# Gate rows spread over the partitions by products with an identity column, in place of 24 one-row transfers

## The chip, the core and the metric

The kernel runs on one core of one Trainium2 chip. The metric is the device time of one execution in microseconds (us). TensorE (PE) multiplies matrices, VectorE (DVE), ScalarE (ACT) and GpSimd (POOL) work element by element, and SyncE (SP) issues all the transfers of this kernel. Each engine takes its own instructions in order and waits for the others by semaphores. PEld is the part of TensorE that loads the stationary operand. TensorE's clock has two levels, 2.4 and 1.2 GHz; the profile gives the granted one as 1.00 and 0.50.

## The reference, cut to what matters

Two blocks of two layers work on 256 latent tokens (x) and 256 context tokens (ctx), each of 1024 features, in float32. The change is in the first block. There the results of a mixer and of a SwiGLU feed-forward (FFN) are normed, multiplied by a gate and added to the stream:

```
m_lat = silu(c) @ ada_w[l] + ada_b[l]          # the same from c_ctx for the context
sh1, sc1, g1, sh2, sc2, g2 = split(m_lat, 6)
x = x + g1 * rmsnorm(y_lat, norm_g[l, 1])      # y_lat: the mixer's result
f = swiglu(rmsnorm(x, norm_g[l, 2]) * (1 + sc2) + sh2, ffn_w_in[l], ffn_w_out[l])
x = x + g2 * rmsnorm(f, norm_g[l, 3])
```

Layer 0 mixes by pooling and a gated recurrence (HGRN) and treats both streams; layer 1 mixes by grouped attention (GQA) and treats the latent stream alone. That makes six gates: g1 and g2 of both streams in layer 0, and g1 and g2 in layer 1. A gate is one row of 1024 values for all tokens of its stream.

## The kernel before

**Weights.** Each large product is three products of split operands (`mm3`, L174 to L177): both operands are cut into a high and a low part. A piece of a weight arrives in a buffer `raw` (transfer at L163), ACT writes its high part `hi` (L151), and DVE, now and then POOL, its low part `lo` (L152). In the first block's layer 0 there are four `raw` buffers and two pairs of `hi` and `lo`; a pair can be rewritten only when TensorE has used it for every token tile.

**Conditions.** The six vectors of a layer lie in a tile `adarows` of 128 partitions by 6 by 256 values (`ada_rows`, L567). Vector v is cut into four pieces of 256 values, and piece j of stream s is on the single partition 32 j + s. Of layer 0, the first norm's scale and shift are made at the start, and the gate g1 and the second norm's two during the mixer; g2 of layer 0 and all of layer 1 are summed on DVE (`ada_apart`, L540: two passes over each piece `adaw` of the weight, L554 and L556, for two streams) while the FFN of layer 0 runs, and one product (L562) adds such a sum over the partitions.

**Gates.** `ada_gate` (L632) makes one gate for use by a token tile, whose tokens are on the partitions. The row must therefore stand on all 128 partitions. It loads the post-norm's gain, a row of DRAM on every partition, into a tile `big`, and copies the four pieces by transfers that read one partition's 256 values 128 times, once for each partition. DVE then multiplies gain and gate:

```
for j in range(4):
    p = 32 * j + s
    self.dma(gate[:, j * 256:(j + 1) * 256], self.adas[l][p:p + 1, 3 * n + 2].unsqueeze(1).to_broadcast([1, P, 256]))
self.V.scalar_tensor_tensor(gate, gain, 32.0, gate, op0=ALU.mult, op1=ALU.mult)
```

The transfers are L638 and the multiplication is L639. The six calls come in pairs at three places: L1652 before the product with `ab_w_out` that ends the HGRN mixer (call it the first place), L1689 in the FFN of layer 0 (second place), and L1713 before the product with `att_w_out` that ends the GQA mixer (third place). The gate is used by `post` (L680): L685 squares a half of a tile's y on ACT, and L686 multiplies y by the gate on DVE. `post_end` (L689) and `prenorm` (L672) follow: the sum of squares becomes a factor (L658, and a power on POOL, L270), L693 adds to the stream, L649, L651 and L652 norm the new stream, L239 transposes it on TensorE, and the scaled transposes are split for the next layer's products.

**Order.** The program's order gives each instruction a priority, and a scheduler sets each engine's order from priorities and estimated times; what it sets is fixed. PSUM tiles are given out by tag in the program's order: the tag `tr` has two banks, `C` one, `A` three and `B` two. All transfers stand in SP's one queue.

Of the kernel before, what the change touches and what calls it, by code (L numbers as in the profile page):

```python
# [17 lines left out]
P = 128  # L18
D = 1024
# [6 lines left out]
# ---------------------------------------------------------------- constants of the shapes alone  # L26
def _constants():
    """One [128, n] float32 array of masks and tables, and where each part lies in it."""
# [3 lines left out]
    # blocks of 1, 2, 4, .. in pairs: the two halves of each pair against each other  # L32
# [49 lines left out]
class Kern:  # L82
    def __init__(self, tc, d, es, stop=None):
        self.tc, self.nc, self.d, self.es, self.stop = tc, tc.nc, d, es, stop
        self.V, self.S, self.G, self.T = tc.nc.vector, tc.nc.scalar, tc.nc.gpsimd, tc.nc.tensor
        self.dma = tc.nc.sync.dma_start
        self.cp = self.pool("cp", 1)
        self.xt = self.pool("xt", 1)
        self.rp = self.pool("rp", 1)
        self.mm = self.pool("mm", 1, space=PSUM)  # L90
        self.n = 0
        self.post_ss, self.post_y = {}, {}
        # two places for a transposed activation [128, 8, 256], as hi and lo
        self.xh, self.xl = (self.t(self.xt, [P, 2, 8, 256], n, F32R) for n in ("xh", "xl"))
        self.place = 1
# [17 lines left out]
    def ps(self, shape=(P, 512), tag="A"):  # L113
        """A bank of PSUM. A tag's tiles are given out in the order of the program."""
        return self.t(self.mm, list(shape), tag, bufs=self.BANKS[tag])
# [7 lines left out]
    def buffers(self, es, raw, split):  # L123
        """Buffers for pieces of weights, for the products that follow."""
# [7 lines left out]
    def low(self):  # L132
        """Instructions that only fill the gaps of others."""
# [6 lines left out]
    def later(self, n):  # L140
        """Instructions that may come after n of those that follow."""
# [4 lines left out]
    # ------------------------------------------------------------ splitting and products  # L146
    spread = False

    def split(self, hi, lo, src, pool=False):
        """hi + lo == src exactly, each with 12 significant bits."""  # L150
# [3 lines left out]
    def piece(self, shape, srcs, perm=None):  # L154
        """A piece of a weight, split: srcs(raw) -> [(part of raw, dram)], of half the piece's second dimension at a time."""
# [24 lines left out]
    def among(self, steps):  # L180
        """A step after each of the products that follow: those of few columns cost the array
        little more than their weights, which are loaded during the others."""
# [6 lines left out]
    def wcols(self, w, c0, n):  # L189
        """[1024, n] columns of a weight as pieces of four chunks of K."""  # L190
# [3 lines left out]
    def tok_major(self, xT, tiles, pcs, n, done, tag=None):  # L194
        """done(tile, psum [tokens, n]) of x @ w for pieces of w, each used for all tiles in turn
        (two at a time if a tag is given)."""
# [12 lines left out]
    def by_tile(self, xT, tiles, jobs, tag=None):  # L209
        """For jobs (pieces of w, columns, done) as in tok_major: all of a tile's products, then the next one's."""  # L210
# [10 lines left out]
    def feat_major(self, xT, w, c0, blocks, done, tag="B"):  # L221
        """done(i, psum [128 features, 256 tokens]) of (x @ w)^T for blocks of 128 columns from c0,
        the banks of tag in turn."""
# [12 lines left out]
    def transposes(self, ps, src, blocks):  # L236
        """ps[:, i] = (block i of src)^T"""
# [3 lines left out]
    def to_xT(self, x, hi, lo, tl, n=8):  # L241
        """Token-major x [128, n*128] into columns tl*128.. of hi, lo [128, n, 256]."""
# [16 lines left out]
    def tiles_of(xT):  # L259
        """Access by (token tile, chunk) to [(hi, lo)] by stream."""  # L260
# [6 lines left out]
    # ------------------------------------------------------------ small things  # L267
# [19 lines left out]
    def bcast(self, pool, row, n, tag, bufs=None):  # L287
        """A row of DRAM on every partition."""
# [4 lines left out]
    def columns(self, rows, name, pool=None):  # L293
        """Rows of 128 values (pairs: dram [r, 128], r) as columns of a [128, r] tile."""
# [13 lines left out]
    def log1p(self, y, n):  # L308
        """log(1 + y) for y in [0, 1]: 2 atanh(y / (2 + y))."""
# [29 lines left out]
    # ------------------------------------------------------------ SwiGLU  # L339
    def ffn(self, xT, streams, gate, up, down, splits, hpool, finish, ypool=None, each=None):  # L340
        """finish(tile, half, psum or None, sbuf or None) gets each [128, 512] of the result.
        splits: units of 256 hidden features in each round; the rounds before the last are
        summed in ypool."""
# [6 lines left out]
        for r, nu in enumerate(splits):  # L350
            hs, first = [], []
            for u in range(nu):
# [12 lines left out]
                # the first two units' products of one tile give the other one's norm time  # L365
# [29 lines left out]
    def up_tile(self, xT, tl, pcs, h, pool):  # L395
        """256 hidden features of a token tile, tokens on partitions and then transposed."""
# [14 lines left out]
    def up_one(self, xT, pcs, h, pool):  # L411
        """256 hidden features of a stream, features on partitions."""
# [12 lines left out]
    def up_both(self, pcs, h, pool, apart, each):  # L425
        """256 hidden features of both streams, features on partitions; apart: one stream after the other."""
# [22 lines left out]
    def down(self, lhs, tiles, wv, nk, out):  # L449
        """out(tile, half, psum [128, 512]) of a^T-chunks @ w; wv: [128, nk, 1024] of DRAM."""  # L450
# [35 lines left out]
    # ------------------------------------------------------------ setup  # L486
    def setup(self):
# [7 lines left out]
        # silu of both conditions, as columns, padded to the 32 columns of a tile of the array  # L495
# [11 lines left out]
    def gains(self):  # L507
        """The pre-norms' gains and other vectors as columns."""
# [12 lines left out]
    # ------------------------------------------------------------ adaLN vectors  # L521
    def ada(self, l, vectors):
        """Some of the six vectors (1024 outputs each), a piece of the weight a step."""
# [16 lines left out]
    def ada_apart(self, pool, pick, l, vectors, streams):  # L540
        """As ada, with only the sum over the partitions on TensorE."""
# [25 lines left out]
    def ada_rows(self, l):  # L567
        """The vectors' rows, the bias in them: a fourth j of vector v on the 32 partitions from 32 j."""
# [6 lines left out]
    def ada_first(self):  # L575
        """Scale and shift of the first pre-norm, 256 features a step: step(g) makes their rows and
        returns the last instructions on PE and DVE; columns(g) then adds them to scale and shift."""
# [9 lines left out]
        def step(g):  # L587
            ps = self.ps((P, 2, 256))
            for v in (1, 0):
                # a chunk of K in four adds up on the same 32 partitions  # L590
# [22 lines left out]
    def ada_cols(self, l, v):  # L613
        """[128, chunk, stream] of vector v, in PSUM."""
# [7 lines left out]
    def ada_pre(self, l, n):  # L622
        """Scale (times sqrt(D)) and shift of the pre-norm n (0, 1), as columns [128, chunk, stream]."""
# [8 lines left out]
    def ada_gate(self, l, n, s):  # L632
        """Gate times the post-norm's gain (and sqrt(D)) of one stream, on every partition [128, 1024]."""
        gate = self.t(self.gp, [P, D], "gg", bufs=2)
        gain = self.bcast(self.sp, self.d["norm_g"][l, 2 * n + 1], D, "big")
        for j in range(4):
            p = 32 * j + s
            self.dma(gate[:, j * 256:(j + 1) * 256], self.adas[l][p:p + 1, 3 * n + 2].unsqueeze(1).to_broadcast([1, P, 256]))  # L638
        self.V.scalar_tensor_tensor(gate, gain, 32.0, gate, op0=ALU.mult, op1=ALU.mult)  # L639
        return gate  # L640

    def normed(self, x):
        """x over its root sum of squares (eps within)."""
# [11 lines left out]
    def rroot(self, ss):  # L655
        """(sum of two + D eps)^-1/2: the reciprocal root mean square over sqrt(D) = 32."""
# [4 lines left out]
    def modulated(self, src, c0, sc, sh, s, hi, lo, tl):  # L661
        """Four transposed chunks of src, scaled and shifted by feature, split."""
# [9 lines left out]
    def prenorm(self, x, sc, sh, s, hi, lo, tl):  # L672
        """RMS norm of a token tile, scaled and shifted by feature, transposed and split."""
# [6 lines left out]
    def post(self, tl, half, y, gg, dst):  # L680
        """First step of x + gg * rms-normed y, for a half of a tile's y."""
# [13 lines left out]
    # ------------------------------------------------------------ block 1, layer 0: pooling and HGRN  # L695
    def hgrn_mixer(self, xT, q0, fill):
        """Returns cat[stream] = (hi, lo) of the concatenated result [128, 8, 256], transposed."""
        d, V, S, G, T = self.d, self.V, self.S, self.G, self.T
        w = d["ab_w_in"][0]
        with self.scope("hg") as hp:  # L700
            # lower bound of the forget gate: the softmax over the first axis, its first row
# [17 lines left out]
            def project(pr):  # L719
                """q, f and k of heads 2 pr, 2 pr + 1; then f's products in the places of q and k."""  # L720
                wv = w.rearrange("(k p) f -> p k f", p=P)
                c0 = 512 + pr * 256
                # [direction (for A and F the second first), stream, head, token]
                q = {}
                A, B, F = (self.t(hp, [P, 2, 2, 2, 256], n) for n in "ABF")
                for part in range(3):
# [8 lines left out]
                    # the streams apart where one of them is wanted first  # L735
# [26 lines left out]
            def levels(q, A, B, F):  # L762
                """The scores within each tile, [key, tile, head, query]."""
# [11 lines left out]
                # A: q times the products from its block's edge; B: k times the products to its block's edge  # L775
                for l in range(7):
# [4 lines left out]
                    # the first half of each pair of one direction and the second of the other's: in the order of  # L781
                    # the tokens (some tiles of a stream's heads), and all of a stream by direction
# [121 lines left out]
    def headnorm(self, pool, o, nh, gain, gate, out):  # L904
        """out = RMS norm over each head's 128 of o [128, nh, 128], times gain and gate (overwritten)."""
# [11 lines left out]
    # ------------------------------------------------------------ block 1, layer 1: grouped attention  # L917
    def gqa_mixer(self, xT, wider):
# [3 lines left out]
        with self.scope("ga", side="right") as hp:  # L922
# [20 lines left out]
            def normed(ps, nh, nm, tl, tag):  # L943
                """RMS norm by head of ps [128, nh*128], its gain, and the rotation for the latent tiles."""
# [81 lines left out]
    # ------------------------------------------------------------ block 2: shared  # L1026
# [3 lines left out]
    def post_ln(self, pool, i, n, x, scale, xT):  # L1030
        """Returns finish(tile, half, psum): x <- LN(alpha x + scale psum), and its transpose into xT; and the new x."""
# [27 lines left out]
    def ple_part(self, pool, i):  # L1059
        """p @ wp in SBUF."""  # L1060
# [37 lines left out]
    def prepare(self, pool):  # L1098
        """The small parameters of both mixers."""
# [19 lines left out]
    # ------------------------------------------------------------ block 2, layer 0: windowed attention and RG-LRU  # L1119
# [710 lines left out]
```

## Time and profile before

| what | value |
|---|---|
| median of 3 runs | 2246.57 us (2244.58 to 2249.68) |
| profiled execution, first to last instruction | 2246.9 us (a time of its own is not given beside the span) |
| PE busy | 2099.7 us, 93% of the span |
| DVE busy | 1367.5 us, 61% |
| ACT busy | 970.4 us, 43% |
| DMA queue of SP | 353.56 MB, 52.9% of 16 engines' span |
| mean granted clock of TensorE | 0.973 |

TensorE is busy nearly all the time, so the profile is read from the short stretches in which it isn't: in the row of PE over 40 slices the low digits, and the rows of waits that say who ended them. The clock falls to 0.50 in some of these stretches, which makes the products after them slower for a while.

### The profile page before, as it was taken

Reading aid. Unit: us, or ns where it says so; the run is one execution under the profiler, and the core shown is the slowest. Engines: PE = TensorE matmul, PEld = TensorE weight load, DVE = VectorE, ACT = ScalarE, POOL = GpSimd, SP = SyncE. Lnnn points to the kernel's source line nnn. Section 1 sums busy time; section 2 is a strip of 40 time slices with the busy share of each in tenths; the row PEclk is TensorE's granted clock in tenths of the full one; section 3 lists DMA queues with packets and bytes.
Section 4 is the critical chain, followed back from the end, with each engine's and each line's share of the span. In section 5 each row is a group of like instructions: output and inputs, shape, how many; then the busy total and the mean of one; then the engine's idle time right before and its main releaser. Section 6 shows DMA issues by size and latency. Waiting matters only on the chain. (4 is left out here: it accounts for less than half of the span.)

```text
span 2246.9 us, 33927 instructions
## 1 busy us (share of the span) xinstructions
PE 2099.7 (93%) x13130; PEld 1824.3 (81%) x13130; DVE 1367.5 (61%) x2424; ACT 970.4 (43%) x1904; POOL 254.1 (11%) x248
## 2 busy tenths in 40 slices
PE   7999969599999885999999998999999998999998
PEld 4787858487888754998899787998899878879987
DVE  4746558567534873654655648554765487876546
ACT  4323343132323553544544366544454355445443
POOL 0524100000000211000100212000100055220000
PEclk9999989799999997999999999999999999999999
DMA  9632547768423406656665525765566554226652
GB/s 310 220 95 76 129 70 210 162 205 265 146 86 97 138 31 101 196 181 189 193 187 187 170 80 178 220 181 190 165 201 183 161 161 123 66 95 207 187 188 103
DMA packets 242396, 355.71 MB, mean 158 GB/s; under 512 B 14816, under 2 KB 188476, under 8 KB 242108
## 3 DMA queue, kind: packets, MB, share of 16 engines
q1 hardware_dynamic: 242236, 353.56, 52.9%
q8 instruction: 103, 1.69, 0.3%
q14 instruction: 57, 0.47, 0.1%
HBM read 349.31 MB, written 1.05 MB: 156 GB/s over the span
## 5 line engine op out<-in xcount | busy, mean ns | idle before, releaser
L151 ACT ACTIVATE hi<-raw 128x512 fp32r<-128x512 f32 (+1 forms) x1072 | 601.0, 617 | 733.1 <-issue 357.3
L152 DVE TENSOR_TENSOR lo<-raw,hi 128x512 fp32r<-128x512 f32 x1006 | 671.2, 710 | 379.5 <-ACT hi L151 377.5
L176 PE MATMUL B<-xh,hi 128*128 128x256 f32 (+1 forms) x1200 | 368.7, 308 | 1.6 <-ACT r L1137 1.4
L176 PE MATMUL B<-xl,hi 128*128 128x256 f32 (+1 forms) x1200 | 367.8, 307 | 1.0 <-DVE xl L152 0.9
L176 PE MATMUL B<-xh,lo 128*128 128x256 f32 (+1 forms) x1200 | 368.1, 307 | 0.0
L176 PE MATMUL A<-xh,hi 128*128 128x256 f32 (+1 forms) x1008 | 305.0, 303 | 3.1 <-ACT a L1385 2.9
L176 PE MATMUL A<-xh,lo 128*128 128x256 f32 (+1 forms) x1008 | 303.8, 302 | 0.7 <-DVE lo L152 0.7
L176 PE MATMUL A<-xl,hi 128*128 128x256 f32 (+1 forms) x1008 | 303.9, 302 | 0.0
L176 PEld LDWEIGHTS B<-xh,hi 128*128 128x128 f32 x1200 | 230.9, 193 | 11.9 <-ACT r L1137 1.6
L176 PEld LDWEIGHTS B<-xl,hi 128*128 128x128 f32 x1200 | 231.0, 192 | 11.3 <-DVE xl L152 1.9
L176 PEld LDWEIGHTS B<-xh,lo 128*128 128x128 f32 x1200 | 230.6, 192 | 10.6 <-issue 1.5
L176 PEld LDWEIGHTS A<-xh,hi 128*128 128x128 f32 x1008 | 193.7, 192 | 11.6 <-ACT a L1385 3.1
L176 PEld LDWEIGHTS A<-xh,lo 128*128 128x128 f32 x1008 | 193.5, 192 | 8.4 <-DVE lo L152 2.0
L176 PEld LDWEIGHTS A<-xl,hi 128*128 128x128 f32 x1008 | 193.8, 192 | 6.2
L176 PE MATMUL B<-hi,xh 128*128 128x512 f32 (+1 forms) x464 | 171.0, 369 | 5.8 <-DVE r L1044 2.7
L176 PE MATMUL B<-lo,xh 128*128 128x512 f32 (+1 forms) x464 | 168.8, 364 | 0.0
L176 PE MATMUL B<-hi,xl 128*128 128x512 f32 (+1 forms) x464 | 168.6, 364 | 0.0
L270 POOL TENSOR_TENSOR pow<-rv,mhalf 128x1 f32<-128x1 f32 (+2 forms) x54 | 42.6, 789 | 1050.2 <-DVE rv L275 506.8
L152 POOL TENSOR_TENSOR lo<-raw,hi 128x512 fp32r<-128x512 f32 x66 | 96.0, 1468 | 468.9 <-ACT hi L151 437.5
L176 PE MATMUL A<-hi,hh 128*128 128x512 f32 x308 | 122.8, 399 | 0.0
L176 PE MATMUL B<-hi,hh 128*128 128x512 f32 x308 | 122.5, 398 | 0.0
L176 PE MATMUL B<-hi,hl 128*128 128x512 f32 x308 | 122.1, 396 | 0.0
(437 smaller groups left out, 3416.2 us busy)
## 6 DMA issues: line engine op xcount, KB each, us to landing
adaw<-in_ada_w SPq DMA_DIRECT2D x96, 512.0 KB, 5.0
raw<-in_ffn_wg SPq DMA_DIRECT2D x88, 512.0 KB, 4.7
raw<-in_ffn_wu SPq DMA_DIRECT2D x88, 512.0 KB, 4.5
raw<-in_ffn_wd SPq DMA_DIRECT2D x88, 512.0 KB, 4.0
raw<-in_ffn_w_in SPq DMA_DIRECT2D x88, 256.0 KB, 4.4
raw<-in_ffn_w_in SPq DMA_DIRECT2D x44, 512.0 KB, 4.4
raw<-in_ab_w_in SPq DMA_DIRECT2D x38, 512.0 KB, 4.4
raw<-in_ffn_w_out SPq DMA_DIRECT2D x38, 512.0 KB, 4.3
```

Source lines behind the costliest of these rows:

```text
L151: self.S.activation(hi, src, AF.Copy)
L152: (self.G if pool else self.V).tensor_tensor(lo, src, hi.bitcast(F32), op=ALU.subtract)
L176: self.T.matmul(ps, l, r, start=first and i == 0, stop=last and i == 2)
L270: self.G.tensor_tensor(r, x, exponent_tile[:, :x.shape[1]], op=ALU.pow)
```

## The change

`ada_gate` no longer copies by transfers. A column of the identity matrix, repeated 128 times along the free axis, is the stationary operand of a product whose moving operand is one vector of `adarows` (128 partitions by 256 values). The column has its one at partition 32 j + s, so each of the 128 result rows is that partition's row. Two products fill a bank of the tag `tr`; DVE multiplies the gain by that bank, half a gate at a time, and writes the gate. Four products and two multiplications of 128x512 take the place of four transfers and one multiplication of 128x1024, six times. Comments and blank lines that differ are left out here.

```
     def ada_gate(self, l, n, s):
         gate = self.t(self.gp, [P, D], "gg", bufs=2)
         gain = self.bcast(self.sp, self.d["norm_g"][l, 2 * n + 1], D, "big")
-        for j in range(4):
-            p = 32 * j + s
-            self.dma(gate[:, j * 256:(j + 1) * 256], self.adas[l][p:p + 1, 3 * n + 2].unsqueeze(1).to_broadcast([1, P, 256]))
-        self.V.scalar_tensor_tensor(gate, gain, 32.0, gate, op0=ALU.mult, op1=ALU.mult)
+        for c in range(2):
+            ps = self.pst((P, 2, 256))
+            for j in range(2):
+                p = 32 * (2 * c + j) + s
+                self.T.matmul(ps[:, j], self.ident[:, p:p + 1].to_broadcast([P, P]), self.adas[l][:, 3 * n + 2], start=True, stop=True)
+            sl = slice(c * 512, c * 512 + 512)
+            self.V.scalar_tensor_tensor(gate[:, sl], gain[:, sl], 32.0, ps.rearrange("p j n -> p (j n)"), op0=ALU.mult, op1=ALU.mult)
         return gate
```

In the changed file the products are L641 and the multiplications L643; lines after them are numbered four higher than before. The scheduler moves the rest at three places.

DVE at the first place, before (`xl<-tr` is the split of the mixer's last transposes, `lo<-raw` that of the third piece of `ab_w_out`, y the product's result):

```order
L915 TENSOR_TENSOR r_170_980<-ht_2281,r_170_980 128x256
L152 TENSOR_TENSOR xl_68<-tr_2305,xh_67 128x4x128
L639 SCALAR_TENSOR_TENSOR gg_2329<-big_2330,gg_2329 128x1024
L639 SCALAR_TENSOR_TENSOR gg_2337<-big_2338,gg_2337 128x1024
L152 TENSOR_TENSOR lo_2388<-raw_2389,hi_2387 128x512 x2
L152 TENSOR_TENSOR lo_2388<-raw_2395,hi_2387 128x512 x2
L686 TENSOR_TENSOR y_455_2479<-A_2415,gg_2329 128x512
```

And DVE there after:

```order
L919 TENSOR_TENSOR r_170_980<-ht_2281,r_170_980 128x256
L643 SCALAR_TENSOR_TENSOR gg_2329<-big_2330,tr_2332 128x512
L152 TENSOR_TENSOR xl_68<-tr_2305,xh_67 128x4x128
L643 SCALAR_TENSOR_TENSOR gg_2329<-big_2330,tr_2336 128x512
L643 SCALAR_TENSOR_TENSOR gg_2340<-big_2341,tr_2343 128x512
L643 SCALAR_TENSOR_TENSOR gg_2340<-big_2341,tr_2347 128x512
L152 TENSOR_TENSOR lo_2394<-raw_2395,hi_2393 128x512 x2
L152 TENSOR_TENSOR lo_2394<-raw_2401,hi_2393 128x512 x2
L690 TENSOR_TENSOR y_459_2485<-A_2421,gg_2329 128x512
```

The multiplications stand at the same place, ahead of `lo`, but wait for products (PSUM tiles `tr`) and not for transfers. The eight products stand in TensorE's order beside the transposes `tr_2305`; at the third place the eight stand right behind the last products of the attention.

SP's queue at the second place, before (`raw` are pieces of `ffn_w_out`, `adaw` pieces of the condition's weight):

```order
L163 DMA raw_3466<-in_ffn_w_out 128x2x512
L638 DMA gg_5476<-adarows_124_719 128x1x256 x3
L163 DMA raw_3474<-in_ffn_w_out 128x512
L638 DMA gg_5476<-adarows_124_719 128x1x256
L163 DMA raw_3480<-in_ffn_w_out 128x512
L638 DMA gg_5484<-adarows_124_719 128x1x256
L549 DMA adaw_3370<-in_ada_w 128x1024
L638 DMA gg_5484<-adarows_124_719 128x1x256
L549 DMA adaw_3403<-in_ada_w 128x1024
L638 DMA gg_5484<-adarows_124_719 128x1x256 x2
L549 DMA adaw_3407<-in_ada_w 128x1024
```

And SP's queue there after:

```order
L163 DMA raw_3472<-in_ffn_w_out 128x2x512
L163 DMA raw_3480<-in_ffn_w_out 128x512
L163 DMA raw_3486<-in_ffn_w_out 128x512
L549 DMA adaw_3376<-in_ada_w 128x1024
L549 DMA adaw_3409<-in_ada_w 128x1024
L549 DMA adaw_3413<-in_ada_w 128x1024
L549 DMA adaw_3446<-in_ada_w 128x1024
```

The same `raw` and `adaw` follow each other with nothing between them. Of the eight products of this pair of gates, one stands here in TensorE's order, behind the products L562; the other seven and all four multiplications move to the end of the FFN.

DVE at the end of the FFN of layer 0, before (y is the sum of the rounds, `sc` and `sh` the next norm's scale and shift):

```order
L388 TENSOR_TENSOR y_0_619_3588<-y_0_619_3588,A_5462 128x512
L627 TENSOR_SCALAR sc_869_5492<-C_5494 128x16
L628 TENSOR_TENSOR sc_869_5492<-sc_869_5492,colsA_155 128x16
L629 COPY sh_870_5493<-C_5499 128x16
L686 TENSOR_TENSOR y_0_619_3588<-y_0_619_3588,gg_5484 128x512
L388 TENSOR_TENSOR y_1_626_3659<-y_1_626_3659,A_5507 128x512
```

And DVE there after:

```order
L388 TENSOR_TENSOR y_0_623_3594<-y_0_623_3594,A_5468 128x512
L643 SCALAR_TENSOR_TENSOR gg_5482<-big_5483,tr_5485 128x512
L643 SCALAR_TENSOR_TENSOR gg_5482<-big_5483,tr_5489 128x512
L627 TENSOR_SCALAR sc_877_5504<-C_5506 128x16
L628 TENSOR_TENSOR sc_877_5504<-sc_877_5504,colsA_155 128x16
L643 SCALAR_TENSOR_TENSOR gg_5493<-big_5494,tr_5496 128x512
L690 TENSOR_TENSOR y_0_623_3594<-y_0_623_3594,gg_5493 128x512
L643 SCALAR_TENSOR_TENSOR gg_5493<-big_5494,tr_5500 128x512
L629 COPY sh_878_5505<-C_5511 128x16
L388 TENSOR_TENSOR y_1_630_3665<-y_1_630_3665,A_5519 128x512
```

Four multiplications now stand between the first y and its use of the gate.

## Rows read from the trace of the kernel before

**Rows 1.** The page's busy time, share and instructions of each engine.

```profile
PE 2099.7 (93%) x13130; PEld 1824.3 (81%) x13130; DVE 1367.5 (61%) x2424; ACT 970.4 (43%) x1904; POOL 254.1 (11%) x248
```

**Rows 2.** PE's waits, whole span: us in total, times, longest.

```profile
PE tr L239 <- DVE big L651: 33.2, 12, 25.9
PE C L562 <- DVE sum L556: 24.1, 1, 24.1
PE A L176 <- DVE lo L152: 15.4, 4, 14.0
PE tr L239 <- DVE r L1054: 8.7, 6, 3.3
```

**Rows 3.** Windows: us, busy (count) PE, PEld, DVE, ACT, POOL; clock, DMA, GB/s.

```profile
270.00:280.00 10.00, 10.00 (x45) 7.99 (x45) 1.01 (x2) 2.79 (x5) 0.00 (x0) 1.00 0.88 119
288.50:302.60 14.10, 0.06 (x2) 0.01 (x1) 1.93 (x4) 2.62 (x6) 0.00 (x0) 0.58 0.69 63
302.60:307.50 4.90, 4.90 (x12) 3.88 (x13) 4.90 (x9) 0.00 (x0) 0.00 (x0) 0.50 0.60 175
404.20:428.20 24.00, 0.00 (x0) 0.00 (x0) 12.30 (x12) 2.33 (x6) 0.00 (x0) 0.55 0.77 151
428.20:433.80 5.60, 5.53 (x24) 2.83 (x25) 4.54 (x8) 0.63 (x1) 0.00 (x0) 0.50 0.55 180
863.00:888.90 25.90, 0.00 (x1) 0.00 (x0) 7.47 (x11) 3.14 (x7) 2.34 (x3) 0.59 0.60 65
888.90:894.60 5.70, 5.65 (x18) 4.81 (x19) 3.53 (x7) 3.17 (x7) 1.28 (x1) 0.50 0.32 95
```

**Rows 4.** DVE in order of time: start, us, instruction [idle before, releaser].

```profile
287.31 1.23 DVE L639 SCALAR_TENSOR_TENSOR gg<-big,gg 128x1024 f32<-128x1024 f32 x1 [15.14 <-DMA gg<-adarows]
300.71 1.23 DVE L639 SCALAR_TENSOR_TENSOR gg<-big,gg 128x1024 f32<-128x1024 f32 x1 [12.18 <-DMA gg<-adarows]
...
386.52 4.87 DVE L556 SCALAR_TENSOR_TENSOR sum<-adaw,cvec,sum 128x1024 f32<-128x1024 f32 x4
408.77 2.48 DVE L556 SCALAR_TENSOR_TENSOR sum<-adaw,cvec,sum 128x1024 f32<-128x1024 f32 x2 [17.38 <-DMA adaw<-in_ada_w]
...
881.14 1.22 DVE L639 SCALAR_TENSOR_TENSOR gg<-big,gg 128x1024 f32<-128x1024 f32 x1 [12.41 <-DMA gg<-adarows]
882.28 1.28 DVE L686 TENSOR_TENSOR y<-A,gg 128x512 f32<-128x512 f32 x2
```

**Rows 5.** SP's queue in order of time, issues merged.

```profile
268.79 23.18 SPq L638 DMA_DIRECT2D gg<-adarows  x8
...
382.89 3.42 SPq L638 DMA_DIRECT2D gg<-adarows  x3
...
404.38 4.98 SPq L638 DMA_DIRECT2D gg<-adarows  x2
...
848.30 24.58 SPq L638 DMA_DIRECT2D gg<-adarows  x8
```

**Rows 6.** Transfers by line: count, KB each, median us from issue to landing.

```profile
gg<-adarows SPq DMA_DIRECT2D x24, 128.0 KB, 10.8
```

**Rows 7.** PE in order of time, four short stretches.

```profile
16.15 1.06 PE L596 MATMUL A<-bias,ident 24*32 24x256 f32 x2
...
847.62 1.89 PE L1014 MATMUL tr<-pT,v 128*128 128x256 f32 x8
...
849.57 0.40 PE L176 MATMUL A<-hi,xh 128*128 128x512 f32 x1
...
857.18 0.39 PE L176 MATMUL A<-hi,xl 128*128 128x512 f32 x1
...
888.95 1.94 PE L239 MATMUL tr<-ident,big 128*128 128x128 f32 x8 [25.95 <-DVE big L651]
```

**Rows 8.** Groups of instructions: busy us, mean ns | idle before, releaser.

```profile
L639 DVE SCALAR_TENSOR_TENSOR gg<-big,gg 128x1024 f32<-128x1024 f32 x6 | 7.3, 1223 | 54.9 <-DMA gg<-adarows 54.9
L1044 DVE SCALAR_TENSOR_TENSOR r<-A,r 128x512 f32<-128x512 f32 x12 | 8.1, 688 | 23.8 <-PE A L176 23.8
```

**Rows 9.** DVE's waits for `adaw` from 335 to 382 us.

```profile
DVE sum L556 <- DMA adaw<-in_ada_w: 2.7, 2, 1.8
```

## The prediction, made before the changed kernel was run

> **What bounds the kernel now.** I read the page's busy times first: TensorE is busy for 2099.7 us of 2246.9 [rows 1], so a change is worth what it takes out of TensorE's 147 idle microseconds, less what it adds to TensorE. Then TensorE's waits over the whole span [rows 2]. Three single waits stand out: 14.0 us for `lo`, 24.1 us for `sum` and 25.9 us for the normed stream `big`; the next largest kind sums to 8.7 us in six waits. The windows place them [rows 3]: 288.5 to 302.6, 404.2 to 428.2 and 863.0 to 888.9, the three places at which gates are made. In each TensorE is idle, and in the 5 to 6 us behind each its clock is 0.50.
>
> DVE's order of time tells why [rows 4]. At the first place DVE waits 15.1 and then 12.2 us for the transfers `gg<-adarows`; the `lo` that TensorE needs stands behind the second multiplication in DVE's order. At the third place it waits the same way before it reaches y. At the second place nobody waits for a gate: DVE waits 17.4 us for `adaw`. SP's queue explains that one [rows 5]: the gate's transfers stand among the pieces of the weights, and each holds the queue for 1 to 5 us (8 in 23.2 us at the first place), so the `adaw` behind them starts late. One such transfer lands 10.8 us after its issue, with 128 KB [rows 6]. From the first issue (268.79) to the second multiplication (300.71) eight of them, 1.05 MB, take 31.9 us, which is 33 GB/s.
>
> The Trainium skill, DMA: Bandwidth & Descriptors, section "Where 436 GB/s comes from", says that for transfers within SBUF the fabric side, 435 GB/s, is what binds. By that rule the eight would take an estimated 2.4 us and could not be what DVE waits for; the trace disagrees by a factor of 13. If the rule held, the last rival below would follow.
>
> **The change, part by part.** Removed: 24 transfers from SP's queue, and the waits that hang on them.
>
> Added on TensorE: 24 products of 128x256. The nearest row is L1014, the same shape in the same type at full clock [rows 7]: four such products (eight records) from 847.62 to the second product behind them at 849.57 take 1.95 us, less one large product of 0.22 (45 in 10 us, [rows 3]), so 0.43 each. From above, the one product in the trace whose stationary operand is an identity column, L596, takes 1.06 us, at a time when the kernel has just started [rows 7]. I take 0.43, since L1014 has the full shape and the same neighbours; the other end would cost 24 x 0.63 = 15 us more. No gain is possible here: TensorE is fully busy around each place.
>
> Added on DVE: 12 multiplications of 128x512 out of PSUM for 6 of 128x1024. L1044, the same operation out of PSUM, takes 0.69 against 1.22 of L639 [rows 8], so 0.16 more for each gate, 1 us in all. At the first and third place DVE has nothing else to do (1.0 us busy in 10, [rows 3]).
>
> First place: the wait of 14.0 goes, because `lo` of the third piece of `ab_w_out` runs as soon as its `hi` is there, long before TensorE asks for it. Behind the wait 12 products take 4.9 us at half clock; at 0.22 they take 2.7, so 2.2 come back. Against it eight products, 3.5 us, which stand in front of the work that TensorE does from 270 on, and one pass of DVE, 0.7 us, for which TensorE waits because `tr` has two banks and the fourth pair of products needs the bank that the transposes beside it used. 14.0 + 2.2 - 3.5 - 0.7 = 12.0.
>
> Second place: with the gate's transfers gone, `adaw` follows when its buffer is free. DVE's work from 386.52 until TensorE can add up stream 0 is 13 passes of 1.22 [rows 4] and two shorter ones of 0.7: 17.3 us, which ends at 403.8. Waits for `adaw` that stay are read from the vector summed before this one, where no gate's transfer was about: 2.7 us [rows 9]. So 406.5 against 404.2, when TensorE is ready: 2.3 of the 24.1 stay. Half of the 5.6 us at half clock comes back, 2.8. One product stays here, 0.4. 24.1 - 2.3 + 2.8 - 0.4 = 24.2. From both sides: no wait for `adaw` at all gives 2.3 more; 1.8, the longest of [rows 9], at each of the five pieces still to come gives 6.3 less.
>
> Third place: the last product of tile A starts at 857.18 [rows 7]. With eight products (3.5) and one pass of DVE (0.7) in front it ends at 861.6. From there the chain over y, the norm and the transposes takes what it took before from 882.28 [rows 4] to 888.95 [rows 7], 6.7 us: transposes at 868.3. Tile B's products end at 863.0 + 4.2 = 867.2, so 1.1 us of waiting stay and 20.6 are gained. At half clock behind it 5.7 us passed; at most 2.8 come back, and I take 2.0, because the transposes must be split before the FFN can start and ACT and DVE do not get faster. 22.6.
>
> End of the FFN of layer 0: seven products now stand on TensorE's path, 3.0 us. The four multiplications, 2.8 us of DVE, stand between the first y and its use; they are hidden because the next y comes 3.0 us later by these products. Without that cover they would cost up to 2.8 more.
>
> Sum: 12.0 + 24.2 + 22.6 - 3.0 = 55.8 us. The profiled span is 2246.9, 0.3 over the median of 2246.57, so I take the sum off the median: 2190.8, about 2191. Nothing downstream should eat it: between the three places and after them TensorE waits little for weights [rows 2].
>
> On the clock: the rows show 16.1 us of TensorE's busy time at 0.50 behind the three waits [rows 3], and I take 7.0 of it back. In the waits themselves the clock is 0.58, 0.55 and 0.59 on the mean, so together with what follows them it stands at 0.50 for 71 us (11.8 + 21.6 + 21.2 in the waits, 16.2 behind them). The Trainium skill, TensorE: Matmul & The Clock Gate, section "Terms", puts the penalty at the throttled time times one minus the ratio, here an estimated 35 us. The trace bears that out only for time in which TensorE has work; the rest is already in the waits.
>
> **The rivals.** (1) The second place keeps its wait: `adaw` is late by its own 512 KB and three buffers, not by SP's queue. For it: the wait names `adaw`. Against it: only 2.7 us of such waits in the vector before, with the same sizes and buffers. Then 24.2 becomes -0.4, and the time 2215.
>
> (2) The products are dearer, 1.06 us each as in L596. For it: only that row has such a stationary operand. Against it: it stands in the first microseconds of the kernel. 2191 + 15 = 2206.
>
> (3) The low clock costs half of all the 71 us in which it stands, so that 35 and not 7 come back with it: 2163. Against it: TensorE has no work in 55 of the 71.
>
> (4) Slower: the gate's transfers are late because weights occupy the engines in front of them, so that with the gates' transfers gone the same instructions are late for `raw` and `adaw`. The three waits stay, and TensorE gets 10.3 us of products and 1.4 of waits for `tr`: 2258. For it: the share of the DMA engines is 0.6 to 0.8 in the waits. Against it: at such a share only 63 to 65 GB/s move at the first and third place, 119 in the window before [rows 3], so it is these transfers that hold the engines. What the change frees is 14.0 + 2.2 + 24.1 + 2.8 + 25.9 + 2.0 = 71 us and what it costs 15; it decides the sign once fewer than 15 of the 71 go.
>
> **How the numbers follow.** Forecast 0.80, by itself 2185 to 2200 (61 us gained where nothing stays of the waits and the clock; nine lost with 6.3 for `adaw` and 2.8 for the uncovered multiplications). Rival 1 0.06, rival 2 0.07, rival 3 0.02, rival 4 0.03, and 0.02 for something that leaves no change. The range reaches from the forecast's best end to rival 2, and 2 us further on both sides, since the three runs lie 2 below and 3 above their median: 2183 to 2208. No change is what lies within 0.2%, about the least that a measurement of this kernel can tell: faster 0.95, same 0.02, slower 0.03.
>
> **What would show it.** No idle stretch of TensorE over 3 us at the three places, and the clock at 1.00 through them; no wait of DVE for a gate; `adaw` at the second place with waits of a few us; L641 with 48 records and 0.43 us a product; the gates of the FFN multiplied at the end of the FFN, with TensorE 3 us later there. The prediction is wrong if a wait of over 5 us stays at a place, above all at the second, if the products take twice what I took, or if time is given back at a place that I have not named.

## The result, and the profile after

The changed kernel takes 2197.01 us (median of four, 2189.62 to 2198.63) against 2246.41: ratio 0.9772, 95% interval 0.9754 to 0.9789. Two later measurements of the same kernel gave 2188.84 (ratio 0.9756, 0.9738 to 0.9774) and 2190.28 (0.9745, 0.9732 to 0.9759). The forecast of 2190.8 stands between them. What follows reads the profiled execution, the shortest of the four: 2189.62 us with a span of 2187.8, 59.1 us shorter than the span before. By the medians the gain is 49.4 us in the first measurement and 57.9 and 56.0 in the later ones.

The page's busy times and PE's waits over the whole span, after, which answer to [rows 1, 2]:

```profile
PE 2103.7 (96%) x13178; PEld 1827.5 (84%) x13178; DVE 1368.1 (63%) x2430; ACT 970.0 (44%) x1904; POOL 255.0 (12%) x248
...
PE tr L239 <- DVE big L655: 10.1, 11, 2.2
PE tr L239 <- DVE r L1058: 8.7, 6, 3.2
PE A L595 <- DMA adaw<-in_ada_w: 6.9, 3, 6.0
```

PE is busy 4.0 us longer and the span is 59 shorter: it is idle time that went. The single waits of 14.0, 24.1 and 25.9 us are gone; the longest wait for `big` is 2.2.

The windows after, at the first place (two), the second (two) and the third (three), answer to [rows 3]:

```profile
266.60:281.60 15.00, 15.00 (x68) 11.86 (x69) 6.70 (x13) 2.96 (x6) 0.70 (x1) 1.00 0.32 106
281.60:298.00 16.40, 16.40 (x74) 13.59 (x73) 7.63 (x13) 6.29 (x16) 0.00 (x0) 1.00 0.42 126
380.00:395.00 15.00, 15.00 (x77) 11.27 (x76) 14.73 (x19) 4.75 (x10) 0.00 (x0) 1.00 0.62 187
395.00:420.00 25.00, 25.00 (x108) 20.11 (x108) 22.74 (x27) 6.91 (x14) 0.00 (x0) 1.00 0.87 291
...
814.00:830.00 16.00, 15.24 (x67) 12.14 (x67) 8.00 (x16) 3.67 (x11) 1.82 (x2) 1.00 0.29 91
830.00:836.00 6.00, 3.83 (x22) 3.19 (x21) 4.08 (x7) 4.59 (x11) 3.10 (x3) 1.00 0.29 89
836.00:842.00 6.00, 5.96 (x49) 5.71 (x48) 5.57 (x11) 5.81 (x16) 0.92 (x1) 1.00 0.55 161
```

At the first two places TensorE does not stop, at the third it pauses for 3.0 us in all, 2.2 of them ahead of the transposes, and the clock is 1.00 in every one of the windows.

DVE in order of time, after: the first place, then the second [rows 4]; and SP's queue at the second place [rows 5]:

```profile
269.50 0.69 DVE L643 SCALAR_TENSOR_TENSOR gg<-big,tr 128x512 f32<-128x512 f32 x1 [0.16 <-PE tr L641]
...
273.34 0.69 DVE L643 SCALAR_TENSOR_TENSOR gg<-big,tr 128x512 f32<-128x512 f32 x1 [0.24 <-PE tr L641]
...
372.12 12.04 DVE L556 SCALAR_TENSOR_TENSOR sum<-adaw,cvec,sum 128x1024 f32<-128x1024 f32 x10
...
386.84 3.67 DVE L556 SCALAR_TENSOR_TENSOR sum<-adaw,cvec,sum 128x1024 f32<-128x1024 f32 x3
```

```profile
372.23 18.63 SPq L549 DMA_DIRECT2D adaw<-in_ada_w  x8
```

The first pair of gates is done 5.7 us after the start of its first product, and ten passes over `adaw` follow each other without a wait. PE at that time, its products at the first place, at the second, at the end of the FFN of layer 0 and at the third place:

```profile
268.38 1.09 PE L641 MATMUL tr<-adarows,ident 128*128 128x256 f32 x4
...
270.37 2.93 PE L641 MATMUL tr<-adarows,ident 128*128 128x256 f32 x12
...
389.70 0.64 PE L562 MATMUL C<-sum,pick 128*32 128x256 f32 x8
...
392.06 0.59 PE L641 MATMUL tr<-adarows,ident 128*128 128x256 f32 x2
...
676.90 1.89 PE L641 MATMUL tr<-adarows,ident 128*128 128x256 f32 x8
...
815.70 3.04 PE L641 MATMUL tr<-adarows,ident 128*128 128x256 f32 x12 [0.48 <-DVE xl L152]
...
832.27 1.07 PE L239 MATMUL tr<-ident,big 128*128 128x128 f32 x8 [2.17 <-DVE big L655]
```

(A product has two records, so x12 is six products.) How the 59.1 us come about is read by pairing the same product of TensorE in both traces and taking the difference of its starts. For example, the transposes that waited at 888.95 [rows 7] start at 832.27, 56.7 earlier. The difference in each stretch, in us:

| stretch (time before) | lead of after | change | forecast |
|---|---|---|---|
| 255 to 266, ahead of all gates | 0.98 | | |
| 271 to 288, behind eight products | -2.69 | -3.67 | -4.2 (3.5 and 0.7) |
| 308 to 320, first place past | 14.06 | +16.75 | +16.2 (14.0 and 2.2) |
| 395 to 401, ahead of the second place | 14.40 | +0.34 | |
| 440 to 450, second place past | 40.70 | +26.30 | +24.2 |
| 717 to 723, end of the FFN of layer 0 | 37.68 | -3.02 | -3.0 |
| 840 to 848, ahead of the third place | 36.47 | -1.21 | |
| 854 to 862, behind eight products | 32.67 | -3.80 | -4.2 (3.5 and 0.7) |
| 896 to 902, third place past | 58.93 | +26.26 | +26.8 (22.6 and 4.2) |
| 2200 to 2228 | 59.33 | +0.40 | |

The four terms measure 13.1, 26.3, -3.0 and 22.5, in sum 58.9 against the forecast 55.8.

### The profile page after: what moved, and what is told of

Read it like the earlier page. It is cut to its first block, busy times and chain, and to the rows that moved or that the text cites. A ratio compares the mean times of both kernels' runs of the same rounds, so it can differ in the third digit from the quotient of the medians.

```text
span 2187.8 us, 34008 instructions
## 1 busy us (share of the span) xinstructions
PE 2103.7 (96%) x13178; PEld 1827.5 (84%) x13178; DVE 1368.1 (63%) x2430; ACT 970.0 (44%) x1904; POOL 255.0 (12%) x248
## 5 line engine op out<-in xcount | busy, mean ns | idle before, releaser
L176 PEld LDWEIGHTS A<-xh,hi 128*128 128x128 f32 x1008 | 193.4, 192 | 11.7 <-ACT a L1389 3.1
L176 PE MATMUL A<-hi,hl 128*128 128x512 f32 x308 | 121.9, 396 | 0.0
```

Source lines behind the costliest of these rows:

```text
L176: self.T.matmul(ps, l, r, start=first and i == 0, stop=last and i == 2)
```

## The experiments

**One place at a time.** Three kernels make one pair of gates by products and leave the other four gates to transfers:

```
         gain = self.bcast(self.sp, self.d["norm_g"][l, 2 * n + 1], D, "big")
+        if (l, n) != (0, 0):
+            for j in range(4):
...
+            return gate
         for c in range(2):
```

The branch holds the four transfers and the multiplication of before. Its condition is `(l, n) != (0, 1)` in the second kernel and `l == 0` in the third.

> Products for the two gates ahead of ab_w_out alone, transfers for the other four. My theory, that each pair of gates pays for itself where it is used: the first place was forecast at 12.0 us and gives 13.0 between the two traces, so 2246.4 - 12.5 = 2234. Rival: the three places share a cause that only goes when all transfers are gone (the clock, or the queue): less than 8 us here. If the 7.4 us between the executions of the changed kernel come from this pair, only 5 to 6.

> Products for the two gates of the first FFN alone. My theory: the second place was forecast at 24.2 with 3.0 given back at the end of that FFN; the traces show 26.4 and 4.1. So 21 to 22 us: 2224 to 2225. Rival 1 of the prediction (adaw late by itself): nothing gained and 3 to 4 us given back, 2250. If the 7.4 us come from this pair: 14 to 15 us gained.

> Products for the two gates of layer 1 alone. My theory: 22.6 us forecast, 22.3 between the traces: 2224. Rival: with the transfers of the first two places kept the wait for the normed stream has another cause (y late): under 10 us. If the 7.4 us come from this pair: 15 us gained.

Measured, beside 2246.73 of before: 2235.02 for the first place alone (ratio 0.9952, 0.9933 to 0.9972), 2227.05 for the second (0.9920, 0.9902 to 0.9937), 2226.90 for the third (0.9921, 0.9905 to 0.9937). Each pair pays at its own place, and the rivals of a shared cause, of a late `adaw` and of a late y fall. PE's longest waits in the kernel with the second place alone:

```profile
PE tr L239 <- DVE big L661: 34.7, 12, 26.2
PE A L176 <- DVE lo L152: 16.0, 5, 13.7
PE tr L239 <- DVE r L1064: 9.0, 6, 3.2
```

The two other waits stand as they were and that for `sum` is gone. Paired with before as above, the first kernel gains 13.1 at its place and the second 26.3 less 3.3. (The first one's profiled execution, 2229.18 us, is the shortest of seven, which reach to 2240.37; it gained another 6.6 us away from its place, so the differences at the places say more here than the time of one execution.) The third gains only 19.0 of the 22.5. In its profiled execution the clock fell twice for 3.4 us in work that the change had made busy (0.50 from 854.3 and from 871.4), which at half speed costs up to 3.4 us, and the six products took 4.53 in place of 3.04:

```profile
853.29 4.53 PE L647 MATMUL tr<-adarows,ident 128*128 128x256 f32 x12 [0.48 <-DVE xl L152]
```

The medians sum to 51.2 us against 57.9 for the three together; the intervals, about 4 us on either side of each, cover that difference, so nothing is to be read into it.

**The same transfers from 128 partitions.** Before's transfers stay where they are, 128 KB each, with every engine's order word for word as before; only the source changes, and the spreading is left out:

```
-self.adas[l][p:p + 1, 3 * n + 2].unsqueeze(1).to_broadcast([1, P, 256])
+self.adas[l][:, 3 * n + 2]
```

> The kernel before with its 24 transfers in the same places of the same queue, of the same 128 KB each and behind the same semaphores, but each partition reads its own 256 values in place of one partition's 256 values being read 128 times; the spreading of the gate over the partitions is left out. My theory, that reading one partition 128 times is what makes them slow: they land like pieces of a weight (eight in about 9 us in place of 32), the three waits go and no product is paid for, 2246 - 71 + 2 for adaw = about 2177, at most 2190. Rival 4 of the prediction (they are late because of the weights ahead of them, or by their number and place in the queue): 2246, give or take 5.

2180.60 us (ratio 0.9702, 0.9684 to 0.9720). The transfers' count, bytes, queue and place among the weights are as before, and all three waits go; rival 4 of the prediction falls. SP issues the first eight in 5.12 us, not 23.18 [rows 5], and DVE waits little for the gates:

```profile
267.00 5.12 SPq L638 DMA_DIRECT2D gg<-adarows  x8
...
273.11 1.23 DVE L639 SCALAR_TENSOR_TENSOR gg<-big,gg 128x1024 f32<-128x1024 f32 x1 [2.73 <-DMA gg<-adarows]
276.15 1.23 DVE L639 SCALAR_TENSOR_TENSOR gg<-big,gg 128x1024 f32<-128x1024 f32 x1 [1.82 <-DMA gg<-adarows]
```

From the first issue to the second multiplication the eight take 9.2 us against 31.9. So it is the source, one partition read 128 times, that made them slow. That each partition now reads from itself is a second difference, which the packets' times below bear on.

**Four partitions read 32 times**, in the place of one read 128 times:

```
+four = self.adas[l].rearrange("(j q) v n -> j q v n", q=32)[:, s, 3 * n + 2]
-self.dma(gate[:, j * 256:(j + 1) * 256], self.adas[l][p:p + 1, 3 * n + 2].unsqueeze(1).to_broadcast([1, P, 256]))
+self.dma(gate[:, j * 256:(j + 1) * 256], four.unsqueeze(1).to_broadcast([4, 32, 256]))
```

> The kernel before, its 24 transfers in the same order and of the same 128 KB, but each reads four partitions' 256 values 32 times in place of one's 128 times; the gates are therefore not the right ones. My theory, that what is slow is reading the same partition over and over (4.0 us a transfer of 128 reads, eight in 31.9 us): four partitions are read beside each other, about 1 us a transfer, all three waits go, 2180 to 2190. Rival (any repeated read of SBUF is slow, whichever partitions it comes from): 2240 to 2250; between them, with the waits cut by half, about 2210.

2218.39 us (ratio 0.9867, 0.9846 to 0.9888): neither; my 2180 to 2190 was wrong. The eight take 26.7 us (268.15 to 294.87). The DMA rows of 268 to 292 us in 40 slices of 0.6 us (busy share of the 16 engines in tenths, then GB/s), before:

```profile
DMA  0959899988887887777967777765443498788887
GB/s 0 102 164 294 362 406 396 155 27 27 27 27 26 27 27 34 31 67 63 87 24 29 27 31 38 58 48 38 46 46 77 41 32 27 26 27 27 27 32 96
```

And with four partitions as the source:

```profile
DMA  9699983242222222222222222222294982222222
GB/s 102 198 341 331 410 328 114 96 108 48 48 46 48 43 46 46 44 46 44 43 48 44 44 46 44 46 46 41 44 106 96 326 290 60 44 50 43 48 44 44
```

In the kernel before, gate transfers run alone from 272.8 us on: in 19 of these 32 slices one partition gives 26 to 34 GB/s with the engines busy for 0.7 to 0.9, in the others 24 to 96. Four partitions, where they run alone, give 41 to 50 with the engines busy for 0.2. So fewer engines moved more, but a second limit came in: few engines did the work. The Trainium skill, DMA: Bandwidth & Descriptors, section "Rules for kernel authors", has a rule for that: a transfer whose outermost dimension, those of size 1 left aside, has a size below 16 is confined to as many engines. By it this source, 4 by 32 by 256, gets four of 16 at most; the share of 0.2, some 3.5 engines, agrees, and the row read 128 times, 1 by 128 by 256, had most of the 16 busy. My experiment thus changed two things, and how fast four partitions are read by 16 engines stays open.

The packet records in the traces say more than these shares. A gate's packet of 1 KB takes 476 ns before (median from 273 to 291 us, where some 12 engines are busy), 81 ns with four partitions (273.5 to 285 us) and 46 ns when each partition reads itself (268 to 277 us). A tenth of the packets before took 46 ns or less, so reading from another partition is not slow by itself. That the engines wait for each other at the one partition fits these numbers; which engine read which partition isn't recorded, so this is argued and not shown.

**The transfers on ACT's queue.**

```
-self.dma(gate[:, j * 256:(j + 1) * 256], self.adas[l][p:p + 1, 3 * n + 2].unsqueeze(1).to_broadcast([1, P, 256]))
+self.nc.scalar.dma_start(gate[:, j * 256:(j + 1) * 256], self.adas[l][p:p + 1, 3 * n + 2].unsqueeze(1).to_broadcast([1, P, 256]))
```

> The kernel before with its 24 transfers issued by ACT in place of SP; all else stands in the same order. My theory, that each of these transfers keeps the DMA engines busy for as long as it takes, whoever issues it: the gates land about as late, the waits of the first and third place stay, and the weights beside them are slowed all the same; the second place may gain a part, 2235 to 2250. Rival (the transfers only hold SP's queue, in which adaw stands behind them): the second place's 24 us go, 2222, and more if the weights at the other places also come earlier.

2237.99 us (ratio 0.9960, 0.9944 to 0.9976), in the range of my theory. PE's waits:

```profile
PE tr L239 <- DVE big L651: 34.1, 12, 26.8
PE C L562 <- DVE sum L556: 16.4, 1, 16.4
...
PE A L176 <- DVE lo L152: 8.8, 4, 7.6
PE A L176 <- ACT hi L151: 6.9, 3, 5.8
```

At the second place 16.4 of the 24.1 us stay, and the third place is as before. At the first one ACT, in order of time, stands in its own issues, so that `hi` is late beside `lo`:

```profile
271.45 22.52 ACTq L638 DMA_DIRECT2D gg<-adarows  x6
294.02 2.19 ACT L151 ACTIVATE hi<-raw 128x512 fp32r<-128x512 f32 x4 [21.97 <-DMA gg<-adarows]
```

The transfers are no quicker from this queue: one lands 12.4 us after its issue (median), against 10.8 [rows 6]. What the 7.7 us less at the second place mean is not as clear as I had planned, because SP still waits there for gates, from 380 to 425 us:

```profile
SPq L549 <- DMA gg<-adarows: 15.7, 3, 7.9
```

In this program an `adaw` counts its landing on a semaphore that a gate's transfer used just before, and SP holds the `adaw` back until that gate has landed: the first three go out at 395.10, 399.96 and 403.69, each within 0.1 us of such a landing. Beside the gates' transfers an `adaw` also lands later, 6.7 us after its issue (median of those recorded) against 4.0 after the change. So how much of the 16.4 us is the engines that the gates occupy and how much is SP held back by them, this run can't tell, and the rival, an order in the queue alone, stays open for the second place.

**Each product twice**, into the same bank:

```
-self.T.matmul(ps[:, j], self.ident[:, p:p + 1].to_broadcast([P, P]), self.adas[l][:, 3 * n + 2], start=True, stop=True)
+for _ in range(2):
+    self.T.matmul(ps[:, j], self.ident[:, p:p + 1].to_broadcast([P, P]), self.adas[l][:, 3 * n + 2], start=True, stop=True)
```

> The changed kernel with each of its 24 products done twice into the same bank. At 0.43 us a product it takes 10.3 us longer than the changed kernel, about 2207; at 1.06 us (rival 2 of the prediction) 25 us, 2222. If the second product of a pair is hidden beside waits that the first one leaves, under 5 us.

2202.79 us (ratio 0.9809, 0.9790 to 0.9828), 14.0 over the changed kernel in another measurement. Paired with that kernel's second profile, the lead changes by 3.4, 3.4 and 3.0 us where the additional products stand, 9.8 in all or 0.41 a product. The other 4 us of that difference lie where no product was added; there the 0.50 stretches behind 1220 us last 6.8 in place of 3.4 us four times. Rival 2's 1.06 us falls.

**The rows through DRAM.** One transfer writes a gate's row (4 KB) to DRAM, one loads it onto all partitions (512 KB); no product:

```
+self.dma(row, self.adas[l].rearrange("(j q) v n -> j q v n", q=32)[:, s, 3 * n + 2])
+self.dma(gate, row.rearrange("j n -> (j n)").rearrange("(o n) -> o n", o=1).to_broadcast([P, D]))
```

> The row of a gate (four partitions of 256 values, 4 KB) is written to DRAM by one transfer and read back from there onto every partition by another, 512 KB as the gain's; no product and no read of one partition 128 times. My theory: such a load takes about 5 us as that of the gain does, so the three waits go as with the products, without their 24 x 0.43 = 10.3 us on TensorE: about 2186, 10 us under the changed kernel. Rival: what counts is the bytes of the gates among the weights (1 MB a pair either way): the waits stay in part, over 2197.

2180.33 us (ratio 0.9702, 0.9685 to 0.9720). Once more, beside the changed kernel on one chip:

> The version that takes the rows through DRAM once more, beside the changed kernel. My theory: 8 to 10 us under it on the same chip (the 24 products and the waits for their banks, 10.5 us between the two traces, less 1 or 2 for later loads). Rival: the 8.5 us between them in two different calls were the chip, and they are within 3.

2177.28 (ratio 0.9688, 0.9675 to 0.9701) against 2190.28: 13 us less, the two intervals apart, and more than the 8 to 10 that I expected. SP at the first place, and DVE's waits for the gates:

```profile
270.42 0.94 SPq L639 DMA_DIRECT2D gg<-row  x2
```

```profile
DVE gg L640 <- DMA gg<-row: 6.0, 2, 3.5
```

The same kind of broadcast, of four times the bytes for each transfer, is quick when its source is DRAM, and no product stands on TensorE's path. Paired with that run of the changed kernel it gains 3.7 us at the first place, 0.9 at the second, 3.0 to 4.7 at the end of the FFN and 3.8 at the third: about the products' price, read a second time. This version beats both kernels.

**The gain multiplied in before the row is written**, once for both streams. `big` holds the gain's four pieces, each on the 32 partitions of its piece of the vector:

```
+self.V.scalar_tensor_tensor(big[:, 256:512], big[:, 0:256], 32.0, self.adas[l][:, 3 * n + 2], op0=ALU.mult, op1=ALU.mult)
+self.grow = big[:, 256:512].rearrange("(j q) n -> j q n", q=32)
-self.dma(row, self.adas[l].rearrange("(j q) v n -> j q v n", q=32)[:, s, 3 * n + 2])
+self.dma(row, self.grow[:, s])
...
-self.V.scalar_tensor_tensor(gate, gain, 32.0, gate, op0=ALU.mult, op1=ALU.mult)
```

> As the version through DRAM, but the gain is multiplied in before the row is written, on the 128 partitions by 256 values where the vector lies: one DVE pass of 256 columns for both streams in place of two of 1024, and no load of the gain onto all partitions (four of 32 KB in place of 512 KB a gate). My theory: DVE and the transfers of the gain are off TensorE's path by now, so it is within 3 us of the version through DRAM. Rival: the multiplications at the end of the first FFN stand on the path, 2 to 4 us faster.

2177.92 us (ratio 0.9690, 0.9674 to 0.9706), within 1 us of the version through DRAM. That is what my theory had, that the six loads of the gain and the six long multiplications lie off the path; with intervals of about 3 us on either side a gain of 2 us would not have been seen.

**The changed kernel again.**

> The changed kernel once more. The profiled execution of it took 2189.6 us, three others 2197.0 to 2198.6, at a granted clock of 0.989 and 0.985 to 0.986. If the 7.4 us are a place at which the kernel itself can fall one way or the other, both levels come again, and the granted clock of the long ones is lower by about 0.004 x 2190 = 9 us of throttled time. If the short one was a chance of that one execution, all are at 2196 to 2199.

> The changed kernel once more, beside the versions without products on the same chip. It stood at 2197 in three of four executions of its first measurement and at 2187 to 2192 in five of the second. If the clock alone makes that difference, a time of 2197 comes with a granted clock of 0.985 or 0.986 and one of 2189 with 0.989 or 0.990; expected 2187 to 2193.

2188.84 (2187.20 to 2192.23, clock 0.987 to 0.990) and 2190.28 (2188.06 to 2191.99). The level of 2197, with its clock of 0.985 to 0.986, did not come back. The first trace and the second differ by 0.6 to 1.6 us at a time, mostly where a stretch at 0.50 stands in one and not in the other (3.4 us from 35.4 and from 49.1 in the second, from 736.4 in the first) or is twice as long (6.8 us from 1299.6 and from 1746.8 in the first). Worked out from the clocks: 0.004 of 2190 us lost at half clock is about 18 us of such stretches (not the 9 that I had put), which cost up to 8.8 us, and 7.4 were seen. No profile of one of the long executions was taken, so that this is their cause is argued and not shown.

## Why the prediction was right, step by step

**What held the engines.** The prediction read the slow transfers as the cause of all three waits, from 33 GB/s in the eight. The transfers from 128 partitions show it: same queue, same bytes, and none of the three waits. The rule weighed there (the Trainium skill, DMA: Bandwidth & Descriptors, section "Where 436 GB/s comes from": the fabric's 435 GB/s binds within SBUF) is not refuted for a source on all partitions, where that kernel moves 332 GB/s, weights included, from 268 to 274 us at a DMA share of 1.02. For one partition's row it fails.

**First place, 12.0 forecast, 13.1 measured.** The wait and the clock give 16.75 (16.2), the products and the bank cost 3.67 (4.2).

**Second place, 24.2 forecast, 26.3 measured.** The term that was mis-sized is "2.3 of the 24.1 stay": with nothing of the gates in the queue SP has eight `adaw` issued in 18.6 us from 372.23, ahead of DVE's need, and the sum over the partitions follows the product before it at once. In the kernel before SP came to them late:

```profile
400.39 0.54 SPq L549 DMA_DIRECT2D adaw<-in_ada_w  x1
...
409.46 20.22 SPq L549 DMA_DIRECT2D adaw<-in_ada_w  x6
```

With the lead of 14.4, 372.23 is 386.6 in that kernel's time. The bound that I gave for no wait, 2.3 more, is nearly what came.

**End of the FFN, -3.0 forecast, -3.0 measured.** Seven products and their hidden multiplications cost what L1014's row said.

**Third place, 22.6 forecast, 22.5 measured.** That the sum agrees so well is partly luck, since small errors cancel: products and bank cost 3.8 (4.2), the clock gives back 2.3 (2.0), and 2.2 us of waiting stay (1.1).

**Products at 0.43 us.** 3.0 us for seven, and 0.41 from the doubled ones. The choice of L1014's row over that of L596 was right.

**Clock, 7.0 of 16.1 taken back.** The lead grows behind the first place's wait from 11.7 to 14.06, which gives 2.35 (2.2), behind the second's from 38.57 to 40.70, 2.1 (2.8), and behind the third's from 56.6 to 58.93, 2.3 (2.0): 6.8 in all. Rival 3, 35 us, would show as a time near 2163; no run of the changed kernel came near it. **Rivals 1, 2 and 4** are excluded by the kernel with the second place alone, by the doubled products and by the transfers from 128 partitions.

**Not foreseen:** between the places 1.2 us were lost and 0.7 gained. Between 770 and 775 us of the time before, the lead falls from 37.3 to 35.0, where the trace of after has a stretch of 3.4 us at 0.50 (from 736.4) and that of before has none; 1.5 of it is back by 840. The three executions at 2197 were not foreseen either, and what made them longer is not shown.

## What to carry to other kernels

A transfer that spreads one partition's row over the others costs far more than its bytes say (eight of 128 KB in 31.9 us, against 9.2 from 128 partitions), and it keeps the DMA engines busy meanwhile; moved to another queue it landed no earlier. Products with an identity column are cheap (0.43 us for 256 columns) but stand on TensorE's path where TensorE is the bound; a row that is known some microseconds ahead is better written to DRAM and loaded from there with a broadcast. When a wait names a transfer that itself looks harmless, look for what stands ahead of it in its queue, and for the transfer whose semaphore it takes over.

## What was not expected of the hardware

Reading one partition over and over ran mostly at 26 to 34 GB/s with the 16 DMA engines busy for 0.7 to 0.9, so that a high share there says nothing of bytes moved; a broadcast of the same kind out of DRAM needed 0.47 us of SP's queue for 512 KB, against 2.9 for 128 KB. And short stretches of 3.4 us at half clock fall at other places from run to run, each worth 0.7 to 1.6 us where TensorE has work, which is most of the difference between the first and the second profile of the changed kernel.
